# Feed-forward first half: the high and low rows of the activations in one 512-column product

## The chip, the cores and the metric

One NeuronCore of a Trainium2 chip runs the whole program. The metric is the device time of one execution in microseconds (us); lower is better. All tensors live in the chip's memory at the start and end of it.

## The reference, cut to what matters

Two layers; each has a feed-forward pass, a mixer (attention) pass and a second feed-forward pass, all on a sequence of 256 tokens with 1024 features. The feed-forward width is 2816.

```python
def swiglu(h, wg, wu, wd):
    return (jax.nn.silu(h @ wg) * (h @ wu)) @ wd

for l in range(DEPTH):
    mod = (silu(c) @ w_ada[l] + b_ada[l])...
    h = pre(x, 0)                    # RMS norm, scaled and shifted by mod
    x = x + 0.5 * mod[:, 0, 2] * swiglu(h, w_ffn_gate[l, 0], w_ffn_up[l, 0], w_ffn_down[l, 0])
    h = pre(x, 1)
    x = x + mod[:, 1, 2] * (merged_mixers(h) @ w_out[l])
    h = pre(x, 2)
    x = x + 0.5 * mod[:, 2, 2] * swiglu(h, w_ffn_gate[l, 1], w_ffn_up[l, 1], w_ffn_down[l, 1])
```

The change is in `h @ wg` and `h @ wu`, the first half of a feed-forward pass.

## The kernel before, in words

**Precision.** Every weight and every activation is held as two numbers, a high part (float32r, the form the matrix engine takes) and a low part (the float32 rest, again as float32r). A product of two such numbers is three matrix products: high by high, low weight by high activation, high weight by low activation. `hH` and `hL` are the normed activations (128 partitions x 8 blocks of features x 256 tokens), `u.H` and `u.L` a unit's weights.

**Units.** The work is a list of units, 128 x 1024 weights each, in the order in which the matrix engine (PE) uses them. In a feed-forward pass (numbered s = 0, 2, 3, 5; the mixers are s = 1, 4) the first half has a gate unit and an up unit for each of 22 blocks of 128 features, in the order gate, gate, up, up. `aform` (L584 to L594) makes the 24 products of a unit, all 256 columns wide, into one half of a PSUM bank `pf`: gate left, up right. In s = 0 the first six blocks are made in another way (`start_pe`, L624, not touched), so 32 units go through `aform`; in the other three passes there are 44, the first two of them in two parts (high, then low). The second half (`run_rows`, L706) multiplies the result with `w_ffn_down` in 22 units of twelve 512-column products; its last four units are done piece by piece together with the residual and the next norm.

**Feeding.** A raw load of 1 MB brings two units (tile `raw`, three buffers, issued by SP). ScalarE (ACT) rounds it to the high part (`wH`, L150), VectorE (DVE) subtracts to get the low part (`wL`, L158). `feed` is called once per step and prepares exactly the unit that lies five ahead of the one PE is to do next; there are six buffers, so `wH` of unit i+5 has to wait until PE has finished unit i-1. An SP load goes out when the last `wL` of the raw tile three loads back is done.

**The modulation vectors.** `silu(c) @ w_ada` is made on the side: 512 KB loads (tile `ada`, two buffers) are multiplied and added on DVE (L283; the first of eight on ACT, L281). `ada_tick` issues them at a pace set by a table, spread over the steps of a pass.

**Order.** The instruction order on each engine is the order of the program text; each engine takes its own in order. A `step` is: `feed`, `ada_tick`, the unit's products, then what is pending from the step before, then the unit's own `post`. Only up units have a post: silu of the gate half (ACT, L652), times the up half (DVE, L653); one step later the high part (ACT, L656) and the low part (DVE, L657) of the result go to `ffH` and `ffL`.

Of the kernel before, what the change touches and what calls it, by code (L numbers as in the profile page):

```python
# [11 lines left out]
F32R = mybir.dt.float32r  # L12
AF = mybir.ActivationFunctionType
ALU = mybir.AluOpType
AX = mybir.AxisListType

P = 128
D = 1024
S = 256
DEPTH = 2  # L20
KB = D // P
# [68 lines left out]
class Trunk:  # L90
# [434 lines left out]
            self.nc.vector.tensor_tensor(self.hL[:, fs, sl], h32[:, fs, :], self.hH[:, fs, sl], op=ALU.subtract)  # L525

    def alloc_h(self, s):
        self.hH = self.sp.tile([P, KB, S], F32R, tag="hH", name=f"hH{s}", bufs=1)
        self.hL = self.sp.tile([P, KB, S], F32R, tag="hL", name=f"hL{s}", bufs=1)

    def gated(self, t, cols, s, p):
        nc = self.nc
# [36 lines left out]
    def step(self, u):  # L569
        self.feed()  # L570
        self.ada_tick()
        u.pe(u)
        self.done()
        if self.pending:
            self.pending()
            self.pending = None
        if u.post:
            self.pending = u.post()

    def flush(self):  # L580
        if self.pending:
            self.pending()
            self.pending = None

    def aform(self, u, out, xh, xl, off=0, part="all"):

        nc = self.nc
        k = u.shape[0]
        cs = slice(off, off + P)
        seq = [(w, xh, kb) for kb in range(k) for w in (u.H, u.L)] + [(u.H, xl, kb) for kb in range(k)]  # L590
        n = len(seq)
        for i in {"all": range(n), "high": range(2 * k), "low": range(2 * k, n)}[part]:
            w, x, kb = seq[i]
            nc.tensor.matmul(out, w[:, kb, cs], x[:, kb, :], start=i == 0, stop=i == n - 1)  # L594

    def col_raw(self, src, widths=((0, 256),)):

        loads = []
        o = 0
        for c, w in widths:  # L600
            loads.append((lambda t, o=o, w=w: t.rearrange("p (k n) -> p k n", k=KB)[:, :, o:o + w],
                          src[:, c:c + w].rearrange("(k p) n -> p k n", p=P)))
            o += w
        return self.add_raw(loads)

    def plan_ffn(self, l, i, s):
        a = self.a
        wg, wu, wd = a["w_ffn_gate"][l, i], a["w_ffn_up"][l, i], a["w_ffn_down"][l, i]
        plan = {"kind": "ffn", "s": s, "in": [], "out": []}
        ps = {}  # L610

        def start_pe(b0, q):

            def pe(u, between=None):
                for i, (w, x) in enumerate(((u.H, self.hH), (u.L, self.hH), (u.H, self.hL))):
                    if between:
                        between(i)
                    for b in range(2):
                        fb = b0 + b
                        if q == 0 and i == 0:  # L620
                            ps[fb] = self.ps(f"pf{s}_{fb}")
                        for up in range(2):
                            for k in range(2):
                                self.nc.tensor.matmul(ps[fb][:, S * up:S * up + S],  # L624
                                                      w[:, 2 * k + up, b * P:(b + 1) * P], x[:, 2 * q + k, :],
                                                      start=q == 0 and not up and i == 0 and k == 0,
                                                      stop=q == 3 and i == 2 and k == 1, skip_group_check=True)
            return pe

        def start_post(b0):  # L630
            def post():
                laters = [up_post(b0 + b)() for b in range(2)]
                return lambda: [f() for f in laters]
            return post

        def gate_pe(fb):
            def pe(u, part="all"):
                if part != "low":
                    ps[fb] = self.ps(f"pf{s}_{fb}")
                self.aform(u, ps[fb][:, :S], self.hH, self.hL, part=part)  # L640
            return pe

        def up_pe(fb):
            return lambda u: self.aform(u, ps[fb][:, S:], self.hH, self.hL)

        def up_post(fb):
            def post():
                nc = self.nc
                p = ps[fb]
                sil = self.sil[:, fb % 3, :]  # L650
                f32 = self.f32[:, fb % 3, :]
                nc.scalar.activation(sil, p[:, :S], AF.Silu)  # L652
                nc.vector.tensor_tensor(f32, p[:, S:], sil, op=ALU.mult)  # L653

                def later():
                    nc.scalar.copy(self.ffH[:, fb, :], f32)  # L656
                    nc.vector.tensor_tensor(self.ffL[:, fb, :], f32, self.ffH[:, fb, :], op=ALU.subtract)  # L657
                return later
            return post

        if s == 0:
            plan["start"] = []
            k4 = lambda t, n: t[:, :4 * n].rearrange("p (k n) -> p k n", k=4)
            for q in range(4):
                us = []
                for c, n in ((512, 256), (0, 512)):
                    r = self.add_raw([(lambda t, up=up, n=n, o=o:
                                       t[:, :4 * n].rearrange("p (k u n) -> p k u n", k=2, u=2)[:, :, up, o:o + 256],
                                       w[256 * q:256 * q + 256, c + o:c + o + 256].rearrange("(k p) n -> p k n", p=P))
                                      for o in range(0, n, 256) for up, w in ((0, wg), (1, wu))], n == 256)  # L670
                    for o in range(0, n, 256):
                        b0 = (c + o) // P
                        us.append(Unit(r, lambda t, n=n, o=o: k4(t, n)[:, :, o:o + 256], (4, 256),
                                       start_pe(b0, q), start_post(b0) if q == 3 else None))
                self.units += us
                plan["start"].append(us)
        for q in range(3 if s == 0 else 0, NF // 2):
            rg, ru = self.col_raw(wg, ((q * 256, 256),)), self.col_raw(wu, ((q * 256, 256),))
            for r, mk in ((rg, gate_pe), (ru, up_pe)):
                for b in range(2):  # L680
                    fb = 2 * q + b
                    view = lambda t, b=b: t.rearrange("p (k n) -> p k n", k=KB)[:, :, b * P:(b + 1) * P]
                    u = Unit(r, view, (KB, P), mk(fb), up_post(fb) if r == ru else None)
                    self.units.append(u)
                    plan["in"].append(u)
        plan["out"] = self.plan_rows(wd, NF)
        return plan
# [20 lines left out]
    def run_rows(self, us, s, xh, xl, early=None):  # L708
# [3 lines left out]
        n = len(us)  # L712
# [7 lines left out]
        for kb in range(n - TAIL):  # L720
            self.feed()
            self.ada_tick()
            for t in range(2):
                for c in HALVES:
                    self.bform(us[kb], kb, t, c, pd[t, c], xh, xl, kb == 0, t == 1 and c == HALVES[1] and kb == n - TAIL - 1)
            self.done()
            self.flush()
        for c in LATE:
            pd[1, c] = self.ps(f"pe{s}_{c[0]}")[:, :c[1]]
        for ch in nxt:  # L730
# [64 lines left out]
    def run_ffn(self, plan, early=None):  # L795
        s = plan["s"]
        if s:
            self.alloc_ffn(s)
        if s:
            us = plan["in"][:2]  # L800
            for u in us:
                self.feed()
                self.ada_tick()
                u.pe(u, "high")
            for u in us:
                u.pe(u, "low")
            self.done(2)
        for i, u in enumerate(plan["in"]):
            if i > 1 or s == 0:
                self.step(u)  # L810
            if s == 0 and i == 8:
                self.bias_loads()
            if s == 0 and i == 16:
                self.bias_table()
        self.flush()
        self.run_rows(plan["out"], s, self.ffH, self.ffL, early)


# [319 lines left out]
    def run_mixer(self, plan):  # L1138
        s, l = plan["s"], plan["l"]
        nc = self.nc  # L1140
# [47 lines left out]
        for i, u in enumerate(sum(plan["br"], [])):  # L1188
# [3 lines left out]
            self.step(u)  # L1192
            for fn, arg in when.get(("br", i), ()):
                fn(arg)
        self.flush()
        self.run_rows(plan["out"], s, self.mH, self.mL)

    def run(self):
        nc, a = self.nc, self.a
        self.pending = None  # L1200
        self.ada_setup()
        self.x = self.cp.tile([P, 2, D], F32, tag="x", name="x")
        plans = []
# [22 lines left out]
        for t in range(2):  # L1226
            self.mean_eps(t)
            r = self.rstd(t, 0)
# [70 lines left out]
        for n, plan in enumerate(plans):  # L1299
            s = plan["s"]  # L1300
# [6 lines left out]
            else:  # L1307
                k = len(plan["in"])
                parts = [k // 4, k // 4, k - k // 4 * 2, NF - TAIL]
            self.pace = sum(([w] * k for w, k in zip(PACE[s], parts)), [])  # L1310
            f = need / sum(self.pace)
# [39 lines left out]
```

## Time and profile before

| | |
|---|---|
| median of 3 runs | 1211.52 us (1210.78 to 1213.77) |
| the profiled execution, its time | 1215.12 us |
| its span on the core | 1213.4 us |
| matrix engine busy / weight loads busy | 97% / 91% |
| VectorE / ScalarE busy | 69% / 51% |
| memory read and written | 285.12 and 3.42 MB, 238 GB/s over the span |

The span is the time from the first to the last instruction of the profiled execution. The page gives the busy time of each engine, the chain of work that ended last, and groups of instructions; the other views used below are the busy time by stretches, the instructions in order of time, and the waits. Ends of matrix products are modelled, so their pace is read from one start to the next.

### The profile page before, as it was taken

How to read it: one execution, taken by the hardware profiler on the slowest of the kernel's cores; microseconds unless marked ns; L12 is line 12 of the kernel's file. 1: busy time of each engine (PE TensorE's matmuls, PEld its weight loads, DVE VectorE, ACT ScalarE, POOL GpSimd, SP SyncE). 2: the span in 40 equal slices, each digit the busy share in tenths (PEclk: the TensorE clock that was granted, in tenths of full speed). 3: DMA queues.
4: the chain of work that ended last, by engine and by line, in shares of the span. 5: the costliest groups of instructions: out<-in, count | busy, mean ns of one | idle time of the engine just before them, and what ended most of it. 6: DMA issues, size and time to landing. Idle time of an engine off the chain costs nothing.

```text
span 1213.4 us, 21101 instructions
## 1 busy us (share of the span) xinstructions
PE 1181.0 (97%) x8765; PEld 1102.9 (91%) x8765; DVE 837.3 (69%) x1087; ACT 616.0 (51%) x953; POOL 19.0 (2%) x38
## 2 busy tenths in 40 slices
PE   6999998899999999999999999999999999999997
PEld 5999986699999899999889999889999998999986
DVE  3677575878889888766577666567766788555544
ACT  5555343556555475444365444346655456444432
POOL 1000000000000000000000000000000000000000
PEclk9999999899999999999999999999999999999999
DMA  9999889698769959876738676748743584556550
GB/s 318 313 303 332 272 308 318 211 314 271 253 230 314 319 176 326 263 243 242 261 112 298 219 242 226 258 157 291 264 149 113 186 276 147 190 178 197 180 176 35
DMA packets 189671, 287.55 MB, mean 237 GB/s; under 512 B 6806, under 2 KB 155496, under 8 KB 189576
## 3 DMA queue, kind: packets, MB, share of 16 engines
q1 hardware_dynamic: 187656, 279.88, 68.8%
q0 software_dynamic: 1776, 6.14, 1.7%
q8 instruction: 68, 1.11, 0.4%
q14 instruction: 27, 0.22, 0.1%
q10 hardware_dynamic: 144, 0.20, 0.0%
HBM read 285.12 MB, written 3.42 MB: 238 GB/s over the span
## 4 chain that ended last, share of the span: by engine, by line
PE 85%; DMA 6%; DVE 3%; ACT 2%; issue 2%; POOL 1%; SPq 0%; POOLq 0%; ACTq 0%; DVEq 0%
PE pf L594 37%; PE pd L706 16%; PE pg L594 12%; PE pq L594 7%; DMA ada<-in_w_ada 5%; PE pb L594 3%; PE pf L624 3%; PE pv L942 2%; DVE acc L283 1%; DVE wL L158 1%; PE adaf L212 1%; DMA first<-in_w_ada 1%; PE psn L488 1%; ACT wH L150 1%; ACT jk L452 0%
## 5 line engine op out<-in xcount | busy, mean ns | idle before, releaser
L158 DVE TENSOR_TENSOR wL<-raw,wH 128x1024 fp32r<-128x1024 f32 (+1 forms) x384 | 461.8, 1211 | 224.8 <-ACT wH L150 224.3
L150 ACT CAST wH<-raw 128x1024 fp32r<-128x1024 f32 (+1 forms) x384 | 393.1, 1040 | 244.5 <-PE pd L706 90.1
L594 PE MATMUL pf<-hH,wH 128*128 128x256 f32 x1312 | 324.5, 285 | 0.4 <-DVE hH L505 0.4
L594 PE MATMUL pf<-hH,wL 128*128 128x256 f32 x1312 | 323.5, 284 | 0.0
L594 PEld LDWEIGHTS pf<-hH,wH 128*128 128x128 f32 x1312 | 253.1, 193 | 1.7 <-issue 0.9
L594 PEld LDWEIGHTS pf<-hH,wL 128*128 128x128 f32 x1312 | 253.5, 193 | 0.2 <-issue 0.2
L594 PE MATMUL pf<-hL,wH 128*128 128x256 f32 x1312 | 183.8, 283 | 0.0
L283 DVE SCALAR_TENSOR_TENSOR acc<-ada,sc,acc 128x1024 f32<-128x1024 f32 x112 | 143.4, 1280 | 40.6 <-DMA ada<-in_w_ada 40.6
L594 PEld LDWEIGHTS pf<-hL,wH 128*128 128x128 f32 x1312 | 169.1, 192 | 0.0
L706 PE MATMUL pd<-wL,ffH 128*128 128x512 f32 x336 | 132.7, 395 | 5.1 <-DVE wL L158 5.1
L706 PE MATMUL pd<-wH,ffH 128*128 128x512 f32 x336 | 132.5, 394 | 0.0
L706 PE MATMUL pd<-wH,ffL 128*128 128x512 f32 x336 | 132.2, 393 | 0.0
L594 PE MATMUL pg<-hH,wH 128*128 128x256 f32 x384 | 96.0, 288 | 0.0
L594 PE MATMUL pg<-hH,wL 128*128 128x256 f32 x384 | 94.0, 283 | 0.0
L652 ACT ACTIVATE sil<-pf 128x256 f32<-128x256 f32 x88 | 33.3, 382 | 98.4 <-PE pf L594 98.4
L706 PEld LDWEIGHTS pd<-wL,ffH 128*128 128x128 f32 x336 | 63.9, 190 | 19.3 <-DVE wL L158 6.2
L706 PEld LDWEIGHTS pd<-wH,ffH 128*128 128x128 f32 x336 | 63.9, 190 | 14.0 <-issue 0.8
L706 PEld LDWEIGHTS pd<-wH,ffL 128*128 128x128 f32 x336 | 64.0, 190 | 13.2
L594 PEld LDWEIGHTS pg<-hH,wH 128*128 128x128 f32 x384 | 73.5, 191 | 2.3 <-issue 0.9
L594 PEld LDWEIGHTS pg<-hH,wL 128*128 128x128 f32 x384 | 73.6, 192 | 0.0
L653 DVE TENSOR_TENSOR f<-pf,sil 128x256 f32<-128x256 f32 x88 | 36.9, 422 | 33.9 <-ACT sil L652 33.9
L594 PE MATMUL pq<-hH,wH 128*128 128x256 f32 x224 | 55.8, 287 | 0.0
(215 smaller groups left out, 1437.2 us busy)
## 6 DMA issues: line engine op xcount, KB each, us to landing
ada<-in_w_ada SPq DMA_DIRECT2D x128, 512.0 KB, 5.4
raw<-in_w_ffn_down SPq DMA_DIRECT2D x44, 1024.0 KB, 4.8
raw<-in_w_in SPq DMA_DIRECT2D x42, 1024.0 KB, 6.1
raw<-in_w_ffn_gate SPq DMA_DIRECT2D x41, 1024.0 KB, 6.1
raw<-in_w_ffn_up SPq DMA_DIRECT2D x41, 1024.0 KB, 5.8
first<-in_w_ada SPq DMA_DIRECT2D x32, 256.0 KB, 6.0
raw<-in_w_out SPq DMA_DIRECT2D x8, 1024.0 KB, 7.1
raw<-in_w_ffn_gate SPq DMA_DIRECT2D x12, 256.0 KB, 6.0
```

The source lines that it names most:

```text
L150: nc.scalar.copy(u.H, u.view(self.raw_tiles[u.raw]))
L158: nc.vector.tensor_tensor(u.L, u.view(self.raw_tiles[u.raw]), u.H, op=ALU.subtract)
L212: self.nc.tensor.matmul(self.first_ps[q % 2][32 * i:32 * i + 32, 0:P], w, src[:, i * P:(i + 1) * P], start=kb in (0, None), stop=kb == KB - 1)
L283: self.nc.vector.scalar_tensor_tensor(acc, src, sc, acc, ALU.mult, ALU.add)
L488: self.nc.tensor.transpose(p[:, i * P:(i + 1) * P], xn[:, fb * P:(fb + 1) * P], self.ident)
L594: nc.tensor.matmul(out, w[:, kb, cs], x[:, kb, :], start=i == 0, stop=i == n - 1)
L624: self.nc.tensor.matmul(ps[fb][:, S * up:S * up + S], w[:, 2 * k + up, b * P:(b + 1) * P], x[:, 2 * q + k, :], start=q == 0 and not up and ...
L652: nc.scalar.activation(sil, p[:, :S], AF.Silu)
L653: nc.vector.tensor_tensor(f32, p[:, S:], sil, op=ALU.mult)
L706: self.nc.tensor.matmul(out, x[:, kb, sl], w[:, 0, hs], start=first and i == 0, stop=last and i == 2)
L942: self.nc.tensor.matmul(out, x[:, 4 * (i % 2) + k, sl], w[:, k, :], start=i % 2 == 0 and j == 0, stop=i % 2 == 1 and j == n - 1)
```

## The change

`hH` and `hL` become the two halves of one tile `hHL` (per feature block 256 high columns, then 256 low ones). A unit of the first half is now eight products of 512 columns (high weights by both halves, into a whole PSUM bank) and eight of 256 (low weights by the high half, into the left half of the bank): `wide`. The gate has a bank `pf` of its own, the up unit a bank `pu`. The two halves of a bank are added by `join`: a copy of the right half on ACT and an addition on DVE. Gate units now have a post too (join, silu). Posts of all units, those of the mixers too, run one step later than before (`drain`). The first two units of s = 2, 3, 5 keep 256-column products; so do `start_pe`, the mixers and the second half.

```diff
     def alloc_h(self, s):
-        self.hH = self.sp.tile([P, KB, S], F32R, tag="hH", name=f"hH{s}", bufs=1)
-        self.hL = self.sp.tile([P, KB, S], F32R, tag="hL", name=f"hL{s}", bufs=1)
+        self.hHL = self.sp.tile([P, KB, 2, S], F32R, tag="hHL", name=f"hHL{s}", bufs=1)
+        self.hH, self.hL = self.hHL[:, :, 0, :], self.hHL[:, :, 1, :]
...
         u.pe(u)
         self.done()
-        if self.pending:
-            self.pending()
-            self.pending = None
+        self.drain()
         if u.post:
-            self.pending = u.post()
+            self.pending.append(u.post)
+
+    def drain(self):
+        todo, self.pending = self.pending, []
+        for f in todo:
+            later = f()
+            if callable(later):
+                self.pending.append(later)
...
+    def wide(self, u, bank, part="all"):
+        one, two = bank[:, :S], bank[:, S:]
+        kbs = range(u.shape[0])
+        both = self.hHL.rearrange("p k c n -> p k (c n)")
+        seq = {"all": [(bank, u.H, both, kb) for kb in kbs] + [(one, u.L, self.hH, kb) for kb in kbs],
+               "high": [(one, u.H, self.hH, kb) for kb in kbs] + [(one, u.L, self.hH, kb) for kb in kbs],
+               "low": [(two, u.H, self.hL, kb) for kb in kbs]}[part]
+        for i, (out, w, x, kb) in enumerate(seq):
+            self.nc.tensor.matmul(out, w[:, kb, :], x[:, kb, :], start=part != "low" and i == 0,
+                                  stop=part != "high" and i == len(seq) - 1, skip_group_check=True)
+
+    def join(self, out, bank):
+        self.nc.scalar.copy(out, bank[:, S:])
+        self.nc.vector.tensor_tensor(out, bank[:, :S], out, op=ALU.add)
...
+        def gate_post(fb):
+            def post():
+                sil = self.sil[:, fb % 3, :]
+                self.join(sil, ps[fb])
+                self.nc.scalar.activation(sil, sil, AF.Silu)
+            return post
...
+        def up_wide_post(fb):
+            def post():
+                f32 = self.f32[:, fb % 3, :]
+                self.join(f32, pu[fb])
+                self.nc.vector.tensor_tensor(f32, f32, self.sil[:, fb % 3, :], op=ALU.mult)
+                return split(fb, f32)
+            return post
```

`split` is the old last step (high part on ACT, low part on DVE). `run_rows` drains once per unit instead of flushing, and the flushes ahead of it are gone.

How the instructions stand, in the first half of s = 3. On PE, one gate unit (`pf_8` and `pf_9` are gate banks), the end of it before and the whole of it now:

```order
L594 MATMUL pf_8_7230<-hH_6586,wH_7128 128x256
L594 MATMUL pf_8_7230<-hH_6586,wL_7130 128x256
L594 MATMUL pf_8_7230<-hL_6587,wH_7128 128x256 x8
L594 MATMUL pf_9_7261<-hH_6586,wH_7160 128x256
L594 MATMUL pf_9_7261<-hH_6586,wL_7162 128x256
```

```order
L612 MATMUL pf_8_6747<-hHL_6181,wH_6610 128x512 x8
L612 MATMUL pf_8_6747<-hHL_6181,wL_6612 128x256 x8
L612 MATMUL pf_9_6773<-hHL_6181,wH_6634 128x512 x8
L612 MATMUL pf_9_6773<-hHL_6181,wL_6636 128x256 x8
L612 MATMUL pu_8_6801<-hHL_6181,wH_6662 128x512 x8
```

24 products of 256 columns became 8 of 512 and 8 of 256. On ACT, four steps (two gates, two ups), before and now (`f` is the product of silu and up, `raw` the loaded weights):

```order
L150 CAST wH_7257<-raw_7099 128x1024
L150 CAST wH_7286<-raw_7099 128x1024
L652 ACTIVATE sil_6711<-pf_8_7230 128x256
L150 CAST wH_7318<-raw_7164 128x1024
L656 CAST ffH_6709<-f_6712 128x256
L652 ACTIVATE sil_6711<-pf_9_7261 128x256
L150 CAST wH_7353<-raw_7164 128x1024
L656 CAST ffH_6709<-f_6712 128x256
```

```order
L617 COPY sil_6305<-pf_8_6747 128x256
L671 ACTIVATE sil_6305<-sil_6305 128x256
L150 CAST wH_6795<-raw_6638 128x1024
L617 COPY sil_6305<-pf_9_6773 128x256
L671 ACTIVATE sil_6305<-sil_6305 128x256
L150 CAST wH_6821<-raw_6695 128x1024
L617 COPY f_6306<-pu_8_6801 128x256
L150 CAST wH_6848<-raw_6695 128x1024
L690 CAST ffH_6303<-f_6306 128x256
L617 COPY f_6306<-pu_9_6828 128x256
L150 CAST wH_6876<-raw_6745 128x1024
L690 CAST ffH_6303<-f_6306 128x256
```

Each silu now stands between a copy and the next unit's `wH`. On DVE, the same four steps now:

```order
L618 TENSOR_TENSOR sil_6305<-pf_8_6747,sil_6305 128x256
L158 TENSOR_TENSOR wL_6797<-raw_6638,wH_6795 128x1024
L618 TENSOR_TENSOR sil_6305<-pf_9_6773,sil_6305 128x256
L158 TENSOR_TENSOR wL_6823<-raw_6695,wH_6821 128x1024
L283 SCALAR_TENSOR_TENSOR acc_2_6394<-ada_6560,sc,acc_2_6394 128x1024
L618 TENSOR_TENSOR f_6306<-pu_8_6801,f_6306 128x256
L684 TENSOR_TENSOR f_6306<-f_6306,sil_6305 128x256
L158 TENSOR_TENSOR wL_6850<-raw_6695,wH_6848 128x1024
L691 TENSOR_TENSOR ffL_6304<-f_6306,ffH_6303 128x256
L618 TENSOR_TENSOR f_6306<-pu_9_6828,f_6306 128x256
L684 TENSOR_TENSOR f_6306<-f_6306,sil_6305 128x256
L158 TENSOR_TENSOR wL_6878<-raw_6745,wH_6876 128x1024
```

Each addition of a gate (L618 into `sil`) stands behind the `wL` of its step; before, there was no instruction for a gate unit on DVE.

## Rows read from the trace of the kernel before

**Rows 1.** The page: busy time, share of the span and instructions of each engine.
```profile
PE 1181.0 (97%) x8765; PEld 1102.9 (91%) x8765; DVE 837.3 (69%) x1087; ACT 616.0 (51%) x953; POOL 19.0 (2%) x38
```
**Rows 2.** The chain that ended last, pieces in order of time: start us, us, what.
```profile
60.65 48.95 PE pf L594 x408
...
124.33 19.39 DMA ada<-in_w_ada
...
433.27 126.94 PE pf L594 x1056
560.20 54.44 PE pd L706 x240
```
**Rows 3.** Busy time by stretches (PE, PEld, DVE, ACT, POOL), granted clock, DMA share, GB/s.
```profile
60.60:155.30 94.70, 94.70 (x776) 92.97 (x775) 66.60 (x86) 45.70 (x71) 1.68 (x2) 1.00 0.93 302
155.30:219.10 63.80, 57.90 (x256) 45.47 (x255) 43.63 (x43) 23.33 (x28) 0.00 (x0) 0.94 0.90 311
...
241.00:404.00 163.00, 163.00 (x1350) 157.14 (x1351) 139.21 (x176) 93.17 (x149) 0.00 (x0) 1.00 0.82 279
```
**Rows 4.** PE in order of time, first half of s = 2: start us, us.
```profile
433.02 0.36 PE L594 MATMUL pf<-hH,wH 128*128 128x256 f32 x1
...
433.34 0.36 PE L594 MATMUL pf<-hH,wH 128*128 128x256 f32 x1
...
439.08 0.28 PE L594 MATMUL pf<-hH,wH 128*128 128x256 f32 x1
```
**Rows 5.** ACT in order of time, two steps of s = 2: start us, us, [idle before].
```profile
488.24 0.38 ACT L652 ACTIVATE sil<-pf 128x256 f32<-128x256 f32 x1 [1.78 <-PE pf L594]
488.52 1.04 ACT L150 CAST wH<-raw 128x1024 fp32r<-128x1024 f32 x1
489.46 0.41 ACT L656 CAST ffH<-f 128x256 fp32r<-128x256 f32 x1
...
492.72 0.41 ACT L656 CAST ffH<-f 128x256 fp32r<-128x256 f32 x1 [0.21 <-DVE f L653]
```
**Rows 6.** DVE in order of time, s = 2.
```profile
444.77 0.42 DVE L653 TENSOR_TENSOR f<-pf,sil 128x256 f32<-128x256 f32 x1
...
489.59 1.23 DVE L158 TENSOR_TENSOR wL<-raw,wH 128x1024 fp32r<-128x1024 f32 x1 [0.51 <-ACT wH L150]
490.73 1.28 DVE L283 SCALAR_TENSOR_TENSOR acc<-ada,sc,acc 128x1024 f32<-128x1024 f32 x1
491.93 0.42 DVE L657 TENSOR_TENSOR ffL<-f,ffH 128x256 fp32r<-128x256 f32 x1
492.26 0.42 DVE L653 TENSOR_TENSOR f<-pf,sil 128x256 f32<-128x256 f32 x1
```
**Rows 7.** ada additions on DVE (L283) by first half: s = 0, 2, 3, 5.
```profile
60.60:155.30 94.70, 16.65 (x13) 1.00 0.93 302
434.00:560.20 126.20, 19.55 (x16) 1.00 0.80 268
626.20:753.20 127.00, 12.79 (x10) 1.00 0.71 238
1016.50:1145.10 128.60, 0.00 (x0) 0.99 0.58 188
```
**Rows 8.** DVE in order of time, s = 0.
```profile
76.08 1.23 DVE L158 TENSOR_TENSOR wL<-raw,wH 128x1024 fp32r<-128x1024 f32 x1 [7.99 <-ACT wH L150]
...
158.59 1.22 DVE L158 TENSOR_TENSOR wL<-raw,wH 128x1024 fp32r<-128x1024 f32 x1
...
214.63 1.22 DVE L158 TENSOR_TENSOR wL<-raw,wH 128x1024 fp32r<-128x1024 f32 x1
```
**Rows 9.** Who waited for whom, 155 to 235 us (PE) and 60 to 235 us (DVE).
```profile
PE pd L706 <- DVE wL L158: 5.1, 2, 4.4
...
DVE acc L283 <- DMA ada<-in_w_ada: 27.2, 12, 6.2
```
**Rows 10.** One stretch late in s = 0, columns as in rows 3.
```profile
210.00:220.00 10.00, 5.75 (x13) 4.07 (x14) 7.17 (x6) 1.84 (x2) 0.00 (x0) 0.58 0.88 288
```

More of the change, by code (lines that the diff above doesn't have):

```diff
@@ L573, in step @@
         self.done()
-        if self.pending:
-            self.pending()
-            self.pending = None
+        self.drain()
         if u.post:
-            self.pending = u.post()
+            self.pending.append(u.post)
[5 more added lines that the diff above has]
+                self.pending.append(later)
     def flush(self):
-        if self.pending:
-            self.pending()
-            self.pending = None
+        while self.pending:
+            self.drain()
     def aform(self, u, out, xh, xl, off=0, part="all"):
@@ L609, in plan_ffn @@
         plan = {"kind": "ffn", "s": s, "in": [], "out": []}
-        ps = {}
+        ps, pu = {}, {}
         def start_pe(b0, q):
@@ L639, in pe, with split, later @@
                     ps[fb] = self.ps(f"pf{s}_{fb}")
-                self.aform(u, ps[fb][:, :S], self.hH, self.hL, part=part)
+                self.wide(u, ps[fb], part)
             return pe
-        def up_pe(fb):
-            return lambda u: self.aform(u, ps[fb][:, S:], self.hH, self.hL)
+        def gate_post(fb):
[4 more added lines that the diff above has]
+            return post
+        def up_pe(fb):
+            def pe(u):
+                pu[fb] = self.ps(f"pu{s}_{fb}")
+                self.wide(u, pu[fb])
+            return pe
+        def up_wide_post(fb):
[5 more added lines that the diff above has]
+            return post
+        def split(fb, f32):
+            def later():
+                self.nc.scalar.copy(self.ffH[:, fb, :], f32)
+                self.nc.vector.tensor_tensor(self.ffL[:, fb, :], f32, self.ffH[:, fb, :], op=ALU.subtract)
+            return later
         def up_post(fb):
@@ L653, in post @@
                 nc.vector.tensor_tensor(f32, p[:, S:], sil, op=ALU.mult)
[L655 to L658, printed above, removed]
+                return split(fb, f32)
             return post
@@ L678, in plan_ffn @@
             rg, ru = self.col_raw(wg, ((q * 256, 256),)), self.col_raw(wu, ((q * 256, 256),))
-            for r, mk in ((rg, gate_pe), (ru, up_pe)):
+            for r, mk, post in ((rg, gate_pe, gate_post), (ru, up_pe, up_wide_post)):
                 for b in range(2):
@@ L682, in plan_ffn @@
                     view = lambda t, b=b: t.rearrange("p (k n) -> p k n", k=KB)[:, :, b * P:(b + 1) * P]
-                    u = Unit(r, view, (KB, P), mk(fb), up_post(fb) if r == ru else None)
+                    u = Unit(r, view, (KB, P), mk(fb), post(fb))
                     self.units.append(u)
@@ L726, in run_rows @@
             self.done()
-            self.flush()
+            self.drain()
+        self.flush()
         for c in LATE:
@@ L807, in run_ffn @@
             self.done(2)
+            self.pending += [u.post for u in us]
         for i, u in enumerate(plan["in"]):
@@ L814, in run_ffn @@
                 self.bias_table()
-        self.flush()
         self.run_rows(plan["out"], s, self.ffH, self.ffL, early)
@@ L1194, in run_mixer @@
                 fn(arg)
-        self.flush()
         self.run_rows(plan["out"], s, self.mH, self.mL)
@@ L1199, in run @@
         nc, a = self.nc, self.a
-        self.pending = None
+        self.pending = []
         self.ada_setup()
```

## The prediction

> **What bounds the kernel now.** I read four views in turn. First the page's busy times: PE is busy for 97% of the span and weight loads for 91%, DVE for 69%, ACT for 51% [rows 1]. So on average PE is the bound; an average hides which stage has how much room beside it. Second, the chain: the first half of s = 2 is one unbroken piece of PE, 126.94 us for 1056 products, and the second half another, 54.44 us for 240 [rows 2]. In s = 0 the chain is PE up to some 120 us and then goes over the loads of `ada`. Third, the stretches: PE is busy for all of 60.6 to 155.3 us and all of the mixer at 241 to 404, while in the second half of s = 0 (155.3 to 219.1) it has gaps and DMA runs at 311 GB/s [rows 3]. Fourth, the order of time on ACT and DVE: in s = 2 ACT stands still before a silu until PE has finished [rows 5], so in steady state ACT and DVE wait for PE, with their five units of lead full. s = 0 is the exception: PE waits there for `wL` twice, 5.1 us, and DVE for `ada` loads 12 times, 27.2 us [rows 9].
>
> **PE's part.** Products of 256 columns start 126.94 / 1056 = 0.1202 us apart [rows 2]. Products of 512 columns start 54.44 / 240 = 0.2268 us apart [rows 2]. Twice 0.1202 less 0.2268 leaves 13.6 ns per pair: what each product costs beside its columns. A unit goes from 24 x 0.1202 = 2.885 us to 8 x 0.2268 + 8 x 0.1202 = 2.776 us, 0.109 us less. Changed are 32 units in s = 0 and 42 in each of s = 2, 3, 5: on PE alone 3.5 + 3 x 4.6 = 17.2 us. The Trainium skill (TensorE: Matmul & The Clock Gate, Back-to-back issue gap) speaks against this size: it gives columns / 2.4 GHz + 2.5 ns, and a unit would then lose 8 x 2.5 = 20 ns, an estimate by that page, 3.2 us in all. The rows show more than five times its fixed cost, and the sum goes by the rows.
>
> **ACT's and DVE's part.** Four steps (gate, gate, up, up) used to hold, beside four `wH` and four `wL`, two each of silu, `f`, `ffH`, `ffL`. Now come four copies on ACT and four additions on DVE. The trace has no such copy or addition; nearest are silu, also a 256-column read of PSUM by ACT (0.38 us, next start after 0.28 [rows 5]), and `f`, a DVE operation on PSUM and SBUF (0.42, next start after 0.33 to 0.34 [rows 6]); I take these. The amount is harmless; the order is not. ACT's silu of a gate now waits for an addition that stands behind `wL` on DVE, `wL` waits for `wH` on ACT, and the next `wH` stands behind the silu. I walk this loop with start-to-start times: `wH` to `wL` 1.07 (488.52, 489.59 [rows 5, 6]); `wL` to the next on DVE 1.14; a DVE result to its reader 0.46 (492.26 to 492.72 [rows 5, 6]); silu to the next `wH` 0.28 [rows 5].
> - Second gate: `wH` to `wL` 1.07, `wL` 1.14, addition to silu 0.46, silu to the next `wH` 0.28: 2.95 us, all in series.
> - First up: 1.07 to its `wL`, then on DVE 1.14, addition 0.46 (the product reads it), product 0.34: 3.0. ACT runs ahead from here.
> - Second up: `wL`, `ffL`, addition, product on DVE: 2.27.
> - First gate of the next pair: `wL`, `ffL`, addition to silu, silu to `wH`: 2.2.
>
> Together 10.4 us for four steps. PE needs 4 x 2.776 = 11.1, so the loop fits, by 0.7, if nothing else is on DVE. Each `ada` addition adds 1.20 us (490.73 to 491.93 [rows 6]) wherever it falls. With more than one in seven steps the loop is slower than PE; the lead is then eaten, and after it PE waits. So the four first halves differ by their `ada` additions [rows 7]:
> - **s = 5**: none. PE keeps its whole gain: -4.5.
> - **s = 3**: 10, of which 9 fall behind the first `wL` of a gate or up post. 36 units from the ninth on (9 x 10.4) and 9 x 1.2 is 104.4 us, against 36 x 2.776 = 99.9: 4.5 us lost. If it starts as s = 2 does (next point), the ninth unit is ready at 449.0 and PE there at 455.7, a lead of 6.7. That covers it: -4, with 0.5 for short waits.
> - **s = 2**: DVE has made the eighth `wL` and is free at 444.77 [rows 6]; now the two gate posts come ahead of it in series, addition to silu 0.46, silu 0.28, copy 0.44, again 0.46 and 0.28, then `wH` to `wL` 1.07: the ninth `wL` starts at 447.8. Then 9 x 10.4 and 14 additions of 1.2 (counted in the new order): the 45th unit's `wL` is done near 559.5. PE alone would be there at 439.08 (third unit [rows 4]) + 42 x 2.776 = 555.7, and is there before the change at 560.2 [rows 2]. Nearly all the gain is gone; four more units carry the loop into the second half, where PE needs only 12 x 0.2268 = 2.72 a unit: +1.
> - **s = 0**: DVE is never held by PE here after 76 us. The eighth `wL` (76.08 [rows 8]) comes 1.8 us later, at 77.9, since two `ffH`, a copy, an addition and a silu now stand ahead of its `wH` (0.63 + 0.44 + 0.46 + 0.28). The 29 units to the 37th are 7.25 x 10.4, plus 14 x 1.2 and 2.2 us for the gate vector and bias table: it is ready at 174, against 158.59 + 1.2 before [rows 8]. PE used it only at about 60.65 [rows 2] + 32 x 2.885 + 4 x 2.72 and 2 us of side products, 166; so PE is 8 us late at this point. What follows is the stretch in which loads are the limit: from the 37th to the 54th `wL` before, 56.0 us (158.59 to 214.63 [rows 8]) at 311 GB/s [rows 3]. Loads are issued when `wL` and additions end, so they shift too. If PE can run at its pace from there (17 x 2.72 = 46 us), s = 0 ends 4 us late; if the loads need the old 56 us, 14. I take +8: up to then the loads were less crowded than now (302 GB/s over the first half [rows 3]), so some have landed early.
>
> **Small parts.** In s = 2, 3, 5 the first eight products now need all eight feature blocks of `hH` 0.12 us apart instead of 0.24; PE waited there already (433.02 to 433.34 for two products [rows 4]): +0.3 each, +1. The mixers keep their products, and PE has no gap in them [rows 3]; their posts come a step later, which takes waits for PE off ACT and is hidden: 0. Bounds: -1 and +2, where a bank is held too long. The removed flushes are hidden behind the row products.
>
> **Sum.** +8 + 1 - 4 - 4.5 + 1 = +1.5 us on the profiled execution of 1215.12 us. That one is 3.6 us above the median of the runs, 1211.52; on the median this makes 1213.0. About 0.3%, 3.6 us, is what a measurement of this kernel can tell from no change, so my forecast is: no change.
>
> **Rivals.**
> - *The lead covers it (faster).* If the loop's base is nearer 9.2 us than 10.4 (a copy or addition starting earlier than walked), additions at the rate of s = 2 (16 in 44 steps [rows 7]) nearly fit PE's 11.1. For it: PE's first half of s = 2 is unbroken now [rows 2], and there are five units in hand. Against: `wH` and silu stand in one queue, so the series of a gate step has no slack to find. Then s = 2, 3, 5 give 3 x 4.5, s = 0 nothing (loads), the start +1: -12.5, 1199. Half of it, 1205, is still faster.
> - *s = 0 pays in full (slower).* Place: loads of s = 0 after 170 us. If they need the old 56 us, +14 there and +7.5 in all: 1219. It decides once s = 0 loses over 10 us. PE's gaps there carry a price of their own: at 210 to 220 us the granted clock fell to 0.58 with PE busy 5.75 of 10 us [rows 10], between the levels of 2.4 and 1.2 GHz; longer gaps mean more products at the lower one.
> - *The wide product gains nothing.* If a 512-column product in this stream costs two narrow ones, 0.240 us, a unit stays at 2.885: s = 3 and 5 give 0, s = 0 and 2 cost what they do above: +10, 1221.5. Against: the second half's 0.2268 [rows 2] is the same kind of product with a new weight each time. The Trainium skill's rule cited above (TensorE: Matmul & The Clock Gate, Back-to-back issue gap) comes close to this rival, with 20 ns left per unit.
>
> **Chances.** Forecast 0.36 (within 0.3%), lead covers it 0.30 (faster), s = 0 in full 0.30, no gain from width 0.04 (slower together 0.34). The range takes the parts' bounds: s = 0 from 0 to +14, s = 2 from -4 to +3, s = 3 from -4.5 to -2, s = 5 from -4.5 to -3.5; it leaves out the full gain and the no-gain case: 1202 to 1221.
>
> **What would show it.** Right: first-half units of s = 5 start 2.78 us apart without a wait of PE; in s = 2 PE's waits for `wL` add up to some 4 us, late in the half; ACT's silu waits for DVE's addition at every gate, about 1.2 us; the 37th `wL` of s = 0 lies near 173 us, and the first mixer starts some 8 us later than now. Wrong: no waits of PE in s = 2 (the loop is shorter than walked), wide products 240 ns apart, or s = 0 ending where it does now (the loads had room to catch up).

## The result, and the profile after

| | before | after |
|---|---|---|
| median of 4 runs | 1211.19 us (1210.78 to 1213.77) | 1229.69 us (1228.37 to 1231.01) |
| the profiled execution / its span | 1215.12 / 1213.4 us | 1231.01 / 1229.3 us |

The change made the kernel slower: ratio 1.0148, 95% interval 1.0129 to 1.0167. The forecast was 1213.0 us with a range of 1202 to 1221; the time lies 8.7 us above the range.

The page's busy times after, against [rows 1]:

```profile
PE 1179.4 (96%) x7501; PEld 1041.0 (85%) x7501; DVE 891.6 (73%) x1251; ACT 662.0 (54%) x1117; POOL 19.0 (2%) x38
```

PE has 1264 products fewer, and its busy time is 1.6 us less, not 17. The largest part of what is missing returns in s = 0, as products stretched or held up: from 60 us to the first mixer PE is busy for 170.2 us, before for 164.8, though it has less to do. Where that happens is read from the chain of work that ended last, by the first product of each stage (start us, us, what). Before, the first mixer, the first half of s = 3, the second mixer and the first half of s = 5 (s = 2 starts in [rows 2]):

```profile
232.05 2.87 PE pv L942 x24
...
626.24 126.95 PE pf L594 x1056
...
816.58 3.06 PE pv L942 x24
...
1016.56 128.57 PE pf L594 x1056
```

After, the same, the starts of s = 2 and of two second halves (`pd`), and two units of s = 2 (at 465.36):

```profile
252.23 2.87 PE pv L987 x24
...
453.44 6.34 PE pf L612 x48
...
465.36 5.59 PE pf L612 x32
...
584.56 52.67 PE pd L750 x231
...
648.83 6.35 PE pf L612 x48
...
835.88 3.07 PE pv L987 x24
...
1035.88 7.79 PE pf L612 x48
...
1160.99 54.44 PE pd L750 x240
```

The differences of these starts give the time by stage:

| stage | before | after | difference | forecast |
|---|---|---|---|---|
| s = 0, to the first mixer | 232.05 | 252.23 | +20.2 | +8 |
| first mixer | 201.2 | 201.2 | 0 | 0 |
| s = 2 | 193.0 | 195.4 | +2.4 | +1 |
| s = 3 | 190.3 | 187.05 | -3.3 | -4 |
| second mixer | 200.0 | 200.0 | 0 | 0 |
| s = 5, first half | 128.57 | 125.11 | -3.5 | -4.5 |

The sum is +15.8 us; the two spans differ by 15.9. (The medians differ by 18.5, since the profiled execution of before lay 3.9 us above its median and that of the change 1.3.) Of the 14.3 us by which this is over the forecast's +1.5, 12.2 stand in s = 0.

Next, the loop of ACT and DVE that the prediction walked. The waits of ACT over the whole execution (us in total, times, longest):

```profile
ACT sil L671 <- DVE sil L618: 131.7, 82, 7.3
ACT ffH L690 <- DVE f L684: 74.1, 63, 3.0
ACT wH L150 <- PE pd L750: 70.5, 45, 3.8
```

ACT waited at every one of the 82 gate silus for DVE's addition, 1.6 us on average; before, it stood there waiting for PE [rows 5]. DVE in order of time, four steps of s = 2 (start us, us, [idle before <- what ended it]):

```profile
485.18 1.22 DVE L158 TENSOR_TENSOR wL<-raw,wH 128x1024 fp32r<-128x1024 f32 x1
...
487.45 1.22 DVE L158 TENSOR_TENSOR wL<-raw,wH 128x1024 fp32r<-128x1024 f32 x1
488.58 1.28 DVE L283 SCALAR_TENSOR_TENSOR acc<-ada,sc,acc 128x1024 f32<-128x1024 f32 x1
...
490.11 0.42 DVE L618 TENSOR_TENSOR sil<-pf,sil 128x256 f32<-128x256 f32 x1
491.95 1.23 DVE L158 TENSOR_TENSOR wL<-raw,wH 128x1024 fp32r<-128x1024 f32 x1 [1.42 <-ACT wH L150]
493.09 1.28 DVE L283 SCALAR_TENSOR_TENSOR acc<-ada,sc,acc 128x1024 f32<-128x1024 f32 x1
494.29 0.42 DVE L618 TENSOR_TENSOR sil<-pf,sil 128x256 f32<-128x256 f32 x1
496.13 1.23 DVE L158 TENSOR_TENSOR wL<-raw,wH 128x1024 fp32r<-128x1024 f32 x1 [1.42 <-ACT wH L150]
...
498.07 1.22 DVE L158 TENSOR_TENSOR wL<-raw,wH 128x1024 fp32r<-128x1024 f32 x1
```

Behind each addition into `sil` DVE stands for 1.42 us: the addition releases the silu on ACT, the silu lets the next `wH` go, and `wH` lets the next `wL` go. From `wL` to `wL` the four steps take 2.27, 4.50, 4.18 and 1.94 us, 12.89; without the two `ada` additions of 1.20 that is 10.5 us.

In s = 0, DVE again: the eighth `wL`, two places in the middle, the 37th and the 54th.

```profile
76.88 1.23 DVE L158 TENSOR_TENSOR wL<-raw,wH 128x1024 fp32r<-128x1024 f32 x1 [1.42 <-ACT wH L150]
...
147.66 1.28 DVE L283 SCALAR_TENSOR_TENSOR acc<-ada,sc,acc 128x1024 f32<-128x1024 f32 x1 [4.67 <-DMA ada<-in_w_ada]
...
157.60 1.28 DVE L283 SCALAR_TENSOR_TENSOR acc<-ada,sc,acc 128x1024 f32<-128x1024 f32 x1 [3.75 <-DMA ada<-in_w_ada]
...
180.30 1.23 DVE L158 TENSOR_TENSOR wL<-raw,wH 128x1024 fp32r<-128x1024 f32 x1 [1.42 <-ACT wH L150]
...
231.80 1.22 DVE L158 TENSOR_TENSOR wL<-raw,wH 128x1024 fp32r<-128x1024 f32 x1
```

The 37th unit is ready 21.7 us later than before (158.59 [rows 8]), the 54th 17.2 us later (214.63). Busy time by stretches, columns as in [rows 3], before and then after:

```profile
60.00:180.00 120.00, 120.00 (x895) 113.41 (x894) 85.36 (x106) 59.38 (x88) 1.68 (x2) 1.00 0.92 302
```

```profile
60.00:180.00 120.00, 109.22 (x568) 90.09 (x568) 81.64 (x120) 56.66 (x105) 1.68 (x2) 0.96 0.79 254
...
182.00:188.00 6.00, 0.64 (x3) 0.21 (x3) 5.87 (x9) 4.00 (x8) 0.00 (x0) 0.85 0.85 316
188.00:193.00 5.00, 5.00 (x14) 3.94 (x14) 5.00 (x6) 1.66 (x2) 0.00 (x0) 0.50 0.83 281
```

In these 120 us PE loses 11 us, and the DMA queues move 48 GB/s less: 5.8 MB that have to be moved later. Neither ACT (57 of 120 us busy) nor DVE (82) is full; the time goes into the waits between them.

### The profile page after: what moved, and what is told of

Its sections match the earlier page's. It is cut to its first block, busy times and chain, and to the rows that moved or that the text cites. A ratio compares the mean times of both kernels' runs of the same rounds, so it can differ in the third digit from the quotient of the medians.

```text
span 1229.3 us, 19038 instructions
## 1 busy us (share of the span) xinstructions
PE 1179.4 (96%) x7501; PEld 1041.0 (85%) x7501; DVE 891.6 (73%) x1251; ACT 662.0 (54%) x1117; POOL 19.0 (2%) x38
## 4 chain that ended last, share of the span: by engine, by line
PE 76%; DVE 9%; DMA 6%; ACT 4%; issue 4%; POOL 1%; POOLq 0%; SPq 0%; ACTq 0%; DVEq 0%
PE pd L750 16%; PE pf L612 15%; PE pu L612 14%; PE pg L599 11%; PE pq L599 7%; DMA ada<-in_w_ada 4%; DVE wL L158 3%; PE pb L599 3%; PE pv L987 2%; DVE acc L283 2%; ACT wH L150 2%; PE pf L648 2%; DMA first<-in_w_ada 1%; DVE ffL L691 1%; PE adag L344 1%
## 5 line engine op out<-in xcount | busy, mean ns | idle before, releaser
L612 PE MATMUL pf<-hHL,wH 128*128 128x512 f32 (+1 forms) x704 | 170.5, 385 | 5.2 <-ACT wH L150 4.7
L612 PE MATMUL pu<-hHL,wH 128*128 128x512 f32 x656 | 165.1, 394 | 1.6 <-ACT wH L150 1.3
L283 DVE SCALAR_TENSOR_TENSOR acc<-ada,sc,acc 128x1024 f32<-128x1024 f32 x112 | 143.4, 1280 | 27.4 <-DMA ada<-in_w_ada 27.4
L612 PEld LDWEIGHTS pf<-hHL,wH 128*128 128x128 f32 x704 | 123.5, 192 | 28.8 <-ACT wH L150 5.3
L599 PE MATMUL pg<-hHL,wH 128*128 128x256 f32 x768 | 145.3, 286 | 0.0
L612 PEld LDWEIGHTS pu<-hHL,wH 128*128 128x128 f32 x656 | 117.9, 189 | 24.1 <-ACT wH L150 3.0
L599 PEld LDWEIGHTS pg<-hHL,wH 128*128 128x128 f32 x768 | 121.9, 192 | 2.3 <-issue 0.9
L671 ACT ACTIVATE sil<-sil 128x256 f32<-128x256 f32 x82 | 34.3, 418 | 131.7 <-DVE sil L618 131.7
L612 PEld LDWEIGHTS pf<-hHL,wL 128*128 128x128 f32 x656 | 90.8, 194 | 6.0
L599 PE MATMUL pg<-hHL,wL 128*128 128x256 f32 x384 | 94.0, 283 | 0.0
L612 PE MATMUL pf<-hHL,wL 128*128 128x256 f32 x656 | 93.0, 286 | 0.0
L612 PE MATMUL pu<-hHL,wL 128*128 128x256 f32 x656 | 91.5, 283 | 1.3 <-DVE wL L158 1.3
L750 PEld LDWEIGHTS pd<-wH,ffH 128*128 128x128 f32 x336 | 63.9, 190 | 18.5 <-DVE f L618 3.2
L750 PEld LDWEIGHTS pd<-wL,ffH 128*128 128x128 f32 x336 | 64.0, 190 | 15.8 <-DVE wL L158 2.8
```

The source lines that it names most:

```text
L283: self.nc.vector.scalar_tensor_tensor(acc, src, sc, acc, ALU.mult, ALU.add)
L612: self.nc.tensor.matmul(out, w[:, kb, :], x[:, kb, :], start=part != "low" and i == 0, stop=part != "high" and i == len(seq) - 1, skip_gro ...
L671: self.nc.scalar.activation(sil, sil, AF.Silu)
L750: self.nc.tensor.matmul(out, x[:, kb, sl], w[:, 0, hs], start=first and i == 0, stop=last and i == 2)
```

## The experiments

Median and ratio to before, from the runs of before on the same chip:

| run | us | ratio, 95% interval |
|---|---|---|
| e1_order | 1213.12 | 1.0002 (0.9991 to 1.0013) |
| e2_s0 | 1231.90 | 1.0154 (1.0138 to 1.0169) |
| e3_s35 | 1204.79 | 0.9931 (0.9917 to 0.9946) |
| e4_later | 1203.84 | 0.9919 (0.9902 to 0.9937) |
| e5_half_before | 1204.65 | 0.9943 (0.9925 to 0.9961) |
| e6_half_after | 1223.98 | 1.0097 (1.0082 to 1.0112) |
| e7_later_s235 | 1202.32 | 0.9920 (0.9906 to 0.9935) |
| e8_silu_later | 1205.01 | 0.9944 (0.9924 to 0.9964) |
| e9_bias11 | 1229.66 | 1.0141 (1.0125 to 1.0157) |
| e10_turn5 | 1226.72 | 1.0127 (1.0103 to 1.0151) |
| e11_bias11_turn5 | 1226.38 | 1.0113 (1.0098 to 1.0128) |
| e12_product_later | 1226.58 | 1.0109 (1.0090 to 1.0129) |
| e13_early_turn5 | 1227.83 | 1.0123 (1.0103 to 1.0144) |
| e14_half_early_turn5 | 1220.20 | 1.0059 (1.0043 to 1.0076) |

**Which part, and which stage.** A set of stages `WIDE` decides where the wide form is used; it is empty in e1, (0,) in e2, (3, 5) in e3.

```diff
-                self.wide(u, ps[fb], part)
+                if s in WIDE:
+                    self.wide(u, ps[fb], part)
+                else:
+                    self.aform(u, ps[fb][:, :S], self.hH, self.hL, part=part)
...
+                    if s not in WIDE:
+                        post = up_post if r == ru else lambda fb: None
```

> All products narrow again (the three-pass form of before, silu and product on PSUM in one post per pair); of the change only the order stays: posts one step later, no flush ahead of the row products. Theory A (two queues: ACT's silu waits for DVE's addition, which stands behind wL, and the next wH stands behind the silu) and theory B (the added copies and additions simply take too much of ACT and DVE): no change, 1211 us, ratio within 0.3% of 1. Theory C (the later posts hold banks or rows and cost the time): most of the 18.5 us is here too, 1222 us or more.

> The wide form only in s = 0, narrow in s = 2, 3, 5. If the stages add up as the two traces read (s = 0 loses 20.2, s = 2 loses 2.4, s = 3 and 5 gain 3.3 and 3.5): 1211.2 + 20.2 = 1231 us. If s = 2 starts later only because of what s = 0 left behind, or s = 0 hands its loss on to later stages, the sum differs from that by more than 3 us.

> The wide form only in s = 3 and s = 5, where few or no ada additions stand on DVE. By the stages of the two traces: 1211.2 - 3.3 - 3.5 = 1204.4 us, ratio 0.994. If the gain of s = 3 came only from a lead that the late s = 0 and s = 2 left behind (loads already landed), 1207 to 1208.

The later posts alone cost nothing (1.0002), so theory C falls. The wide form in s = 0 alone costs what the stage table says (1231.9, expected 1231), and in s = 3 and 5 alone it gains what the table says (1204.8, expected 1204.4). The stages add up: the loss is made in s = 0, and no stage hands much on to another.

**Cutting the loop.** In e4 the gate's silu and the up's product each go out one step after their copy and addition.

```diff
                 self.join(sil, ps[fb])
-                self.nc.scalar.activation(sil, sil, AF.Silu)
+                return lambda: self.nc.scalar.activation(sil, sil, AF.Silu) and None
...
                 self.join(f32, pu[fb])
-                self.nc.vector.tensor_tensor(f32, f32, self.sil[:, fb % 3, :], op=ALU.mult)
-                return split(fb, f32)
+
+                def product():
+                    self.nc.vector.tensor_tensor(f32, f32, self.sil[:, fb % 3, :], op=ALU.mult)
+                    return split(fb, f32)
+                return product
```

> All as in the change, but a gate's silu and an up's product are issued one step after their copy and addition, so ACT never waits at a silu for an addition of the same step; the number of instructions is the same. Theory A: the loop is cut, s = 0 loses under 5 us, s = 2 gains 2 to 4, s = 3 and 5 keep their 3.3 and 3.5: 1201 to 1207 us. Theory B: as the change, 1227 to 1231 us.

1203.8 us, 26 us below the change with the same instructions. Its chain (starts of the first mixer, of s = 2, its second half and s = 3), its first stretch and ACT's wait at the silus:

```profile
231.26 2.87 PE pv L990 x24
...
432.49 6.34 PE pf L612 x48
...
556.15 54.44 PE pd L753 x240
...
622.18 6.34 PE pf L612 x48
```

```profile
60.00:180.00 120.00, 119.33 (x647) 101.37 (x646) 97.04 (x140) 68.47 (x120) 1.68 (x2) 1.00 0.92 306
```

```profile
ACT sil L671 <- DVE sil L618: 9.2, 14, 1.4
```

The wait of 131.7 us has become 9.2. DVE and ACT do more in the same 120 us than in the change (97 and 68 us busy against 82 and 57), and the DMA queues are back at 306 GB/s. The first mixer starts at 231.26, 0.8 before that of before. The first half of s = 2 takes 123.66 us, PE's own pace, and the stage 189.7 instead of 193.0. So theory B, too much work on ACT and DVE, falls; theory A stands.

The two halves of that edit one at a time: e8 has only the silu later, e12 only the product.

> As the change, but of the four posts only the two gates' silus are issued a step later; the ups' products stay with their additions. Theory A (it is ACT's wait at the silu, with wH behind it, that closes the loop): as with both later, 1203 to 1206 us. If the up's series copy, addition, product on DVE closes it as well, something between, 1210 to 1222 us.

> The counterpart of the run with the silus alone later: here only the ups' products go a step later, the gates' silus stay right behind their additions. Theory A (the wait at the silu closes the loop): as the change or up to 3 us better, 1226 to 1231 us. Rival (it is any pair of dependent posts in one step): half of the loss goes, 1214 to 1222 us.

The waits of ACT at the silus, first with the silu later, then with the product later:

```profile
ACT sil L671 <- DVE sil L618: 18.8, 24, 1.4
```

```profile
ACT sil L671 <- DVE sil L618: 154.0, 82, 5.7
```

Moving the silu alone brings 1205.0 us, nearly all; moving the product alone leaves ACT's wait in place, and 1226.6 us, some 3 us less than the change, with an interval that just touches that of the change. The loop is closed at the silu.

In e7 the later posts are combined with a narrow s = 0 (`WIDE` = (2, 3, 5)).

> Narrow in s = 0, wide in s = 2, 3, 5 with silu and product a step later. By the stages of the runs so far: before less 3.3 in each of the three: 1211.2 - 9.9 = 1201.3 us. The run with all wide and later ended s = 0 at 231.3 against 228.3 to 228.8 of the two runs with a narrow s = 0; if that is real and not spread, this one is 2.5 us faster than it, if not, the same 1203.8.

1202.3 us, ratio 0.9920 against 0.9919 for e4: the two can't be told apart. Its first mixer starts at 231.62, as late as in e4 though s = 0 is narrow, so the 228.3 to 228.8 of e1 and e3 is spread and not a gain of the narrow form. These two kernels have the lowest medians of the study, 0.8% below before; the intervals of e3 and e8 overlap theirs.

**What the other 12 us of s = 0 are.** First, whether the loads behind the loop set them. Half of s = 0's `w_ffn_down` is not loaded: each load brings 128 of its 256 rows, which stand in for the other 128; e5 is before with this edit, e6 the change with it.

```diff
-            r = self.add_raw([(lambda t: t.rearrange("p (k n) -> p k n", k=2),
-                               w[q * 256:(q + 1) * 256, :].rearrange("(k p) n -> p k n", p=P))])
+            if half:
+                r = self.add_raw([(lambda t: t[:, :D], w[q * 256:q * 256 + P, :])])
```

> Before, with half of s = 0's row weights not loaded (each 256-row load of w_ffn_down brings its first 128 rows, which stand in for the other 128): 11 loads of 0.5 MB instead of 1 MB, 5.5 MB less, at 311 GB/s 18 us of transfer, with the same work on every engine. It gives the base for the next run. If loads set the end of s = 0 in before, 3 to 10 us less than 1211 (PE's own pace bounds it); if not, no change.

> The changed kernel with the same half of s = 0's row weights not loaded. Theory L (the slow loop asks for loads late in the first half of s = 0, and transfer time lost there can't be made up behind it): with 18 us of transfer less behind it, s = 0 loses against the run before only the loop's own lateness, 8 us or less, and the two kernels stand 5 us or less apart. Rival (the loop itself, waits of PE and the lower clock make the 20 us, loads or no loads): they stand 15 to 19 us apart as the full kernels do.

Theory L falls: 19.3 us lie between the two, and 18.5 with all loads. The start of the first mixer in the chain, the stretch of 60 to 180 us, and the 37th and 54th `wL`, e5 and then e6:

```profile
221.96 2.87 PE pv L945 x24
```

```profile
60.00:180.00 120.00, 120.00 (x896) 113.43 (x895) 91.45 (x112) 59.73 (x88) 1.68 (x2) 1.00 0.90 290
```

```profile
156.34 1.22 DVE L158 TENSOR_TENSOR wL<-raw,wH 128x1024 fp32r<-128x1024 f32 x1
...
204.27 1.22 DVE L158 TENSOR_TENSOR wL<-raw,wH 128x1024 fp32r<-128x1024 f32 x1
```

```profile
245.59 2.87 PE pv L990 x24
```

```profile
60.00:180.00 120.00, 109.06 (x579) 89.67 (x577) 83.33 (x123) 58.74 (x108) 1.68 (x2) 0.99 0.78 241
```

```profile
178.21 1.23 DVE L158 TENSOR_TENSOR wL<-raw,wH 128x1024 fp32r<-128x1024 f32 x1 [1.42 <-ACT wH L150]
...
226.19 1.22 DVE L158 TENSOR_TENSOR wL<-raw,wH 128x1024 fp32r<-128x1024 f32 x1
```

Both kernels gain from the smaller loads, before 10.1 us in s = 0 (232.05 to 221.96) and the change 6.6 (252.23 to 245.59). But the loop asks for the loads, so with it they come late, many or few: e6 moves 49 GB/s less than e5 from 60 to 180 us, as the change did against before. From the 37th to the 54th `wL` both now need 48 us, near the 46 that 17 units take at PE's own pace (17 x 12 products at 0.2268 us), and the 21.9 us by which e6 is late at the 37th are still 21.9 at the 54th: nothing is made up.

Then the waits inside the loop. In e9 the bias table's product and write go out at the 12th unit instead of the 17th; in e10 the transposes of an `ada` sum come five steps after it instead of two, in every pass; e11 has both.

```diff
-            if s == 0 and i == 16:
+            if s == 0 and i == 11:
...
-                        self.soon.append([2, x[1], left])
+                        self.soon.append([5, x[1], left])
```

> The changed kernel with the bias table's product and its write to memory (12 x 128 x 383 values, 2.35 MB) five units earlier in s = 0, at the 12th unit instead of the 17th, where the DMA queues had room (77% busy at 80 to 120 us in the profile of the changed kernel). Theory P (of s = 0's 20 us some 8 are the walk's, some 6 the two waits of 4.7 and 3.8 us for ada that fall into the loop at 143 to 157 us, when the table is written, and some 6 the wait of PE for a transpose of ada sums at 182 to 188 us): the two waits go, 5 to 8 us less, 1222 to 1225 us. Rival (the waits come from the order of the loads, not from the table): they move or stay, 1228 to 1231 us.

> The changed kernel with the transposes of a finished ada sum five steps after their sums instead of two, so PE comes to them when ACT's copy is long done. Theory P: PE's 5.4 us wait goes, and with it some 2 us at the lower clock behind it: 1222 to 1226 us. Rival (PE would have waited for wL at that place anyway, since ACT and DVE are the late ones): 1228 to 1231 us.

> Both edits. Theory P: what is left of s = 0's 20 us is the loop's own lateness, 6 to 10 us: 1215 to 1220 us. If the two waits stand in for each other (the later one only grows when the earlier one goes), no better than the better of the two alone.

Waits of PE at 46 to 252 us in the change, at 60 to 190 us in e9, and at 46 to 252 us in e10 (`adam` is the transpose of a finished `ada` sum, `psn` that of the next normed rows `xn`, `psr` the bias table's product, `rb` a small load that it needs, `pd` a row product):

```profile
PE adam L359 <- ACT acc L355: 5.4, 1, 5.4
PE psn L488 <- ACT xn L475: 4.9, 1, 4.9
...
PE pd L750 <- DVE wL L158: 1.7, 2, 0.9
```

```profile
PE psr L428 <- DMA rb<-in_rel_bias: 12.1, 1, 12.1
```

```profile
PE pd L750 <- DVE wL L158: 7.9, 5, 4.0
```

The earlier table brings nothing (1229.66), and shows something else: PE stood 12.1 us for a small load that the table needs, and the time is the same. That wait came at 94 to 106 us, before the loop had caught up with PE, and cost nothing that the time shows. The later transposes take the 5.4 us wait away; 1226.7 and 1226.4 us are some 3 us less than the change; the interval of e10 still overlaps that of the change, that of e11 lies just below it. So the wait counts for about half its length, between what theory P and its rival gave it, and the two edits together bring nowhere near the 10 to 15 us of theory P. The rival's reason shows in e10's row: PE now stands 7.9 us for `wL` where it stood 1.7. That profiled execution was e10's slowest (1231.9 us, the other three 1226.0 to 1227.0), and its first mixer starts no earlier than in the change.

Last, both limits eased at once. e13 also issues the table's small loads four units earlier (`i == 4` for `i == 8`), e14 has the halved loads as well.

> As the run with the earlier bias table and the later transposes, but the four small loads that the table needs are issued at the 5th unit instead of the 9th, so that PE does not stand 11 to 12 us for one of them. Theory Q (two limits close together in s = 0: the loop up to 190 us, the row loads behind it): the loop ends earlier, and the row loads take over; like the earlier run, 1224 to 1227 us. If that 11 us wait of PE was what kept the gain away: 1215 to 1220 us.

> The same with half of s = 0's row weights not loaded (as in the two earlier runs with that edit). Theory Q: with both limits eased at once the loop's own lateness is left, some 8 us over before with the same loads left out (1204.7): 1211 to 1216 us, so 8 us or more below the changed kernel with only the loads halved (1224.0). Rival (the loop alone, slower than walked, makes the 20 us): 1220 to 1224 us.

e13 takes 1227.8 us, no better than e11, so PE's stand for the small load had kept no gain away. e14 takes 1220.2 us, 3.8 below e6 and 15.5 above e5. That is the rival's number, at its lower edge; theory Q falls. DVE and then ACT in e14, at the place where the table is now written:

```profile
128.66 1.23 DVE L158 TENSOR_TENSOR wL<-raw,wH 128x1024 fp32r<-128x1024 f32 x1 [1.42 <-ACT wH L150]
...
137.37 1.23 DVE L158 TENSOR_TENSOR wL<-raw,wH 128x1024 fp32r<-128x1024 f32 x1 [7.16 <-ACT wH L150]
```

```profile
136.30 1.04 ACT L150 CAST wH<-raw 128x1024 fp32r<-128x1024 f32 x1 [5.63 <-DMA raw<-in_w_ffn_gate]
```

The wait for a late load has moved to 130 us: ACT stands 5.6 us for a raw load, and DVE 7.2 us for the `wH` behind it. The table's write was issued at 130.6 us in the change and took 23.7 us to land, in e14 at 111.9 us and took 22.3; in both the late loads fall within it or end just behind it. The 37th `wL` of e14 starts at 178.42, 1.9 before that of the change. So moving the table moves the wait and doesn't take it out of the loop; no run leaves the write out.

## Why the prediction was wrong

**PE's part: right, a little too large.** 32 products, two units, take 5.59 us (the row at 465.36 of the chain): 2.793 us a unit, not 2.776 (in s = 5 it is 2.79 too). A wide product, less the eight narrow ones at 0.1202, costs 0.229 us where 0.2268 was taken. In s = 3, 42 units by 0.092 gain 3.9, and the start takes 0.6 back (48 products in 6.35 us, against 48 x 0.1202 = 5.77); 3.3 is what is seen. In s = 5 the start stands 2.0 us (7.79 less 5.77) and before stood 1.6 (128.57 less 126.94), so 3.5 is left. By the formula of the Trainium skill (TensorE: Matmul & The Clock Gate, Back-to-back issue gap) a wide product would take 512 / 2.4 + 2.5 = 216 ns and a unit 20 ns less, an estimate by that page. The section gives this formula for an isolated product and, for a stream with a weight load to each product, about 131 ns at 512 columns, so the prediction applied it where the page does not. The trace has 229 ns and 92 ns less per unit, and the measurement decides against both figures here.

**The walk of the loop: right.** Four steps were to take 10.4 us and take 10.5, each `ada` addition adds 1.20. The parts agree too, once they are cut from `wL` to `wL`: the prediction put the 1.07 from `wH` to `wL` with the first up (3.0), where the rows have it with the first gate (3.3 and not 2.2, the up then 1.9). In s = 0 from the eighth to the 37th `wL` the walk comes to 75.4 + 16.8 + 2.2 = 94.4 us, start to start; without the two waits of 4.67 and 3.75 the trace has 103.42 - 8.42 = 95.0. That "DVE is never held by PE here after 76 us" doesn't hold for before: ACT's `wH` waited for PE five times from 76 to 181 us, 8.8 us in all, and DVE behind it. The walk of the new loop doesn't use it. In s = 2 the stage lost 2.4 instead of 1; at 526.8 to 584.6 us PE is busy for 54.57 of 57.80 us, 3.2 us idle where some 4 were expected, though the waits stand at `wH` (1.3 us) and an up's addition (1.7), not at `wL`.

**The failed step: "s = 0: ... I take +8".** The term that failed is the lateness at the 37th `wL`: the walk put the waits of the loop for late loads at nothing. By its terms the 37th `wL` starts at 77.9 + 94.4 = 172.3 us (ready at 174); it started at 180.30, 8.0 later, and that is 8.0 of the 12.2 us missing in s = 0. [rows 9] showed 27.2 us of such waits on DVE at 60 to 235 us, and the chain the stretch at 124 us [rows 2]; before, PE's five units of lead lay over them, and PE was busy for all of 60 to 180 us. With the lead eaten they stand on the path like everything else in the loop: the two waits make 8.4 us (the eighth `wL` came 1.0 earlier than walked, the steps took 0.6 more). This is read from the rows; no run takes the waits out.

The other 4.2 us lie behind the 37th. The forecast let 5.7 of its 13.7 us of lateness be made up, on the ground that "up to then the loads were less crowded than now (302 GB/s over the first half [rows 3]), so some have landed early". The loop issues the loads, so fewer had landed: 254 GB/s instead of 302, and 5.8 MB were left for later. From the 37th to the 54th `wL` the change needs 51.5 us, before 56.0, in the middle of the forecast's 46 to 56; 4.5 us come back, and the tail to the first mixer gives 3.0 away (20.4 us for 17.4; PE waits 4.9 us for `xn` in it). So 13.7 forecast lateness + 8.0 - 4.5 + 3.0 = 20.2. Without half of the row loads that stretch takes 48 us in both kernels (e5, e6), so some 3.5 of the change's 51.5 hang on loads, and the rest lies near PE's own pace. What lengthens the tail stays open.

The range was also narrower than the bounds it names: +14 + 3 - 2 - 3.5, and +2 for the small parts, make +13.5, 1225 and not 1221. The measured time lies above that too.

**The rivals.** "s = 0 pays in full" had the right direction and the right stage, but not the mechanism: it let the loads need the old 56 us behind the 37th `wL`, which took 51.5, and it had nothing for the 8.0 us ahead of it. At +14 and 1219 us its price was too low. The low clock that it named is there (0.50 at 188 to 193 us). "The lead covers it" was wrong for this change; with the silu a step later the time comes out where that rival had it: 1203.8, between 1199 for the full gain and 1205 for half of it. "The wide product gains nothing" is refuted by s = 3 and 5.

## What to carry to other kernels

When an operation is split over two engines that each take their instructions in order, don't put the second half behind the first in the same step: the waiting instruction holds up everything behind it on its queue, and here that was the weight preparation of the next unit. One step of distance between the two turned 1229.7 us into 1203.8 with the same instructions. And where a loop loses its lead, price it with all the waits that the lead used to hide, loads first, and with the loads that it will itself ask for later.

## What was unexpected of the hardware

After PE's wait of 5.4 us at 182 to 188 us the granted clock is 0.50 for the next 5 us (188 to 193), 1.2 of 2.4 GHz: 14 products in the time of 22 at 0.227 us. By these rows a wait of 5.4 us costs some 2 us more than its length there, and yet taking it away brought only about 3 us in all, while PE's waits for `wL` grew (e10).
